# A planner's fetch rule and durations in a fused two-layer generator kernel

## The chip, the cores and the metric

The kernel runs on one core of a Trainium2 chip. The core has several engines that each work through a list of instructions of their own: TensorE (PE: matmuls, with PEld for the weight loads that overlap them), VectorE (DVE), ScalarE (ACT), GpSimd (POOL) and SyncE (SP, which here issues the DMA transfers). They wait for each other through semaphores. The metric is the time of one execution on the device in microseconds (us); lower is better.

## What is computed

Two layers over 1024 latent tokens and 256 context tokens, 1024 channels wide. Each layer normalises and modulates its input, projects it, runs three branches (a Fourier mix F, differential attention A, a bidirectional state-space scan S behind a short convolution), gates them, merges them and adds the result to the stream. The reference, cut to this:

```python
for l in range(DEPTH):
    h_l = rmsnorm(x, norm_w[l]) * (1.0 + sc_l) + sh_l          # and h_c from the context
    (fu, fg, q, k, v, ag, z, xbc, dt, gates) = split(h @ w_in[l])
    s = einsum('bqhmd,bkhmd->bhmqk', q, k) * ATT_QK ** -0.5    # two maps per head
    p = softmax(s); a = p[:, :, 0] - lam * p[:, :, 1]
    att = rmsnorm(einsum('bhqk,bkhe->bqhe', a, v), subln_w) * (1.0 - lam_init)
    xbc = silu(depthwise_conv(xbc, conv_w, conv_b))            # five taps, then two scans
    y_f = (fourier_mix(fu) * silu(fg)) @ w_of
    y_a = (att * silu(ag)) @ w_oa
    y_s = rmsnorm(ssd * silu(z), ssd_norm_w) @ w_os
    g = sigmoid(gates)
    x = x + g_l * ((g[0] * y_f + g[1] * y_a + g[2] * y_s) @ w_out[l])
return rmsnorm(x, norm_f)
```

## The kernel before

**Numbers.** Each fp32 operand of a large product is split into an fp16 part and an fp16 remainder, and three fp16 matmuls add up one product (`acc3`). Tiles of 128 tokens by 128 channels meet in matmuls of 128x512 or 128x256, in one of eight PSUM banks.

**Weights.** There are 40 weight tiles in a layer (`fu01`, `qk0`, `x0`, `of0`, `g10` and so on), 80 in all, each fetched by `fetch` (its calls, like every instruction, are recorded under line 397 of the profile, a helper). A fetch has two halves. For each half a 512-KB load brings fp32 values into one of two `raw` buffers, and ACT squares them; the square's output is only scratch and is written into the weight buffer itself, so it must wait until the buffer's last reader is done. What counts is the sum of squares by row (`s1p`, `s1f` or `s1e`). DVE adds the two halves' sums into `b16`, PE adds these over the 128 rows with a one-column matmul against `ones` (`colsum`), DVE makes a power of two of it (`pow2`), and with this scale ACT writes the fp16 part and DVE the remainder (`split_weights`). Letters p, f and e behind `s1` and `b16` tell the three lists that are fetched in their own order: projections (p), output and merge weights (f), and the gates of the scan branch, `g20` to `g23` (e).

**Space.** A fetched half lies in one of eight buffers `w0` to `w7` (`self.wfree`), or in one of 28 larger arena slots `ar0` to `ar27` (`self.free`), which otherwise hold the activations. `done` gives a half back and calls `prefetch`, which decides what to fetch next. Before the change a tile goes to arena slots only if it belongs to the next layer (`ahead`) or is one of `wo0` to `wo3`, the four tiles of the output weight.

**Order.** The kernel is written as six interleaved lists: m (the branches' own work), p (projections), f (merges and the output step), e (gates of the scan branch, behind all others in priority, so used as filler), g (modulation) and w (weight fetches). A planner in the kernel (`Scheduler`) runs through them once when the program is built. It keeps a clock for each engine, gives each instruction a duration (`cost`) and each pair of engines a lag, and each time issues the instruction that can start first, by priority where several can. What it issues is the order in which each engine then runs. DMA transfers have a model of their own: 475 ns of SP for the issue, at least 1100 ns plus bytes by a rate (360 per ns, 290 for a transpose) to the end, one after the other. `may_place` limits how many PSUM banks a list holds.

**The attention step.** For one tile of 128 queries and one head: scores matmuls into five banks, row maxima on DVE, exponentials on ACT, both maps combined on DVE and ACT to an fp16 pair, a transpose by DMA (`DMA_TRANSPOSE ar<-ar`, on SP's queue), and 30 values matmuls of 128x128 out of the transposed tiles.

**The convolution.** Its input comes from PSUM, ACT makes the first tap, DVE adds four more, ACT and DVE make the activation, and fp32 transposes on PE (`ps<-k,ar`, with the identity in `k`) turn the result for the scan.

Of the kernel before, what the change touches and what calls it, by code (L numbers as in the profile page):

```python
# [18 lines left out]
DRAM = bass.MemoryType.DRAM  # L19
# [47 lines left out]
ESIZE = {F32: 4, I32: 4, F16: 2, BF16: 2}  # L67
# [83 lines left out]
class Scheduler:  # L151
# [54 lines left out]
    def may_place(self, b):  # L206

        n, pend = self.count, self.pending
        keep = 0
        if b.th != 'w':  # L210
            if b.th != 'm' and pend['m']:
                keep += max(0, LEAST[self.barred != set()] - n['m'])
            if b.th != 'p' and pend['p'] + pend['w'] and not n['p'] + n['w']:
                keep += 1
        return self.order[b.th][0] is b and (n[b.th] < MAXB[b.th] or not any(pend[k] for k in 'mpf' if k != b.th)) and len(self.psum) > keep


    def cost(self, eng, name, outs, ins, kw, args):
        n = max(a.free_size() for a in outs + ins)
        if eng == 'PE':  # L220
            if name != 'matmul':
                return args[1].free_size() * NS_PE * 2 + 3.0
            n = args[2].free_size() * NS_PE
            return 3.0 + (n if ESIZE[ins[0].dtype] == 2 else max(4 * n, 213.0))
        if eng == 'ACT':
            aps = len(ins) - 1
            return (51 if ins[0].space == PSUM else 93) + n * NS_ACT + 93 * (aps + len(outs) - 1)
        if eng == 'DVE':
            fast = name == 'tensor_copy' or name == 'tensor_scalar'
            fast = fast and all(a.space != PSUM for a in outs + ins)  # L230
            scal = sum(a.free_size() == 1 for a in ins[1:]) if name in ('tensor_scalar', 'scalar_tensor_tensor') else 0
            return 68 + n * NS_DVE * (0.5 if fast else 1) + 61 * scal
        return 60.0 if name != 'tensor_copy' else 150.0 + 2 * n

    def add(self, eng, name, fn, args, kw):
# [19 lines left out]
        o.tail = 0.0  # L255
        if eng == 'SP':
            a = outs[0]
            o.tail = a.partition_size() * a.free_size() * ESIZE[a.dtype] / (720.0 if ins[0].space != DRAM and a.space != DRAM and name == 'dma_start' else 360.0 if name == 'dma_start' else 290.0)
        self.n += 1
        o.th, o.prio, o.n = self.cur, self.n - self.bias[self.cur], self.n  # L260
# [67 lines left out]
    def step(self):  # L328
# [52 lines left out]
        dur = o.dur  # L381
        self.now = s
        if e == 'SP':
            self.clock[e] = s + 475
            o.end = self.dma = max(self.dma, s + 1100) + o.tail
        else:
            if e == 'PE':
                w = int(s / GATE)
                if w != self.gate[0]:
                    self.gate = [w, 0.0, self.gate[1] if w == self.gate[0] + 1 else 0.0]  # L390
                if self.gate[2] < 0.5 * GATE:
                    dur *= 2
                self.gate[1] += dur
            o.end = self.clock[e] = s + dur
# [20 lines left out]
class Builder:  # L415
    def __init__(self, ctx, tc, A, out, dbg):
# [16 lines left out]
        self.wnext = {k: [(l, n) for l in range(2) for n in v] for k, v in (('p', W_PROJ), ('f', W_MERGE), ('e', W_GATE))}  # L433
        self.ev = set()
        self.block = {}
        self.cur, self.budget, self.held, self.cap = 'p', 0, 0, 99


# [118 lines left out]
    def fetch(self, k):  # L557

        nc = self.nc
        cur, ncur = self.cur, nc.cur  # L560
        self.cur, nc.cur = k, 'w'
        l, name = key = self.wnext[k].pop(0)
        self.whold[k] += 1
        halves, bufs = [], []
        sq = self.small(2)
        raws = []
        for j in range(2):
            if self.wfree:
                buf = self.wfree.pop(0)
                w = self.wbuf[buf]  # L570
            else:
                buf = self.alloc(keep=True)
                self.wborrow += 1
                w = buf.v16(2048).rearrange("p (a c) -> p a c", a=2)
            bufs.append(buf)
            halves.append((w[:, 0], w[:, 1]))
            raw = self.ring("raw", RAW, 1024)
            nc.sync.dma_start(raw, self.A['wt'][l, TILE_IDX[name]][:, j * 1024:j * 1024 + 1024])
            nc.scalar.activation(w[:, 1], raw, AF.Square, accum_out=sq[:, j:j + 1])
            raws.append(raw)  # L580
        inv = self.col("iw", 12)
        self.split_weights(halves, raws, sq, inv)
        self.wcache[key] = [halves, inv, bufs, k]
        nc.close('w')
        self.cur, nc.cur = cur, ncur

    def prefetch(self, want=None):

        idle = self.block.get('f') in {(l, 'z' + b) for l in range(2) for b in ORDER[1:]}
        for k in 'pef' if idle else 'pfe':  # L590
            while self.wnext[k] and self.wnext[k][0][0] < (self.layers if k == 'p' else min(self.layers, self.flayer + 1)):
# [1 line left out]
                ahead = k == 'p' and self.wnext['f'] and l > self.wnext['f'][0][0]  # L593
                left = k == 'f' and self.wnext['e'] and self.wnext['e'][0][0] == l
                lim = 1 if ahead else (0 if idle else 2) if left else WLIM[k] if (self.fetch_p if k == 'p' else self.fetch_f) else 0
                wo = name[:2] == 'wo'
                need = 2 + max(0, self.later) + (0 if (l, name) == want else BOR if wo and self.wborrow < BMAX else 99)
                borrow = (ahead or wo) and len(self.free) >= need
                if self.whold[k] >= lim or len(self.wfree) < 2 and not borrow:
                    break  # L600
                self.fetch(k)
# [4 lines left out]
    def done(self, L, name, half=None):  # L606

        e = self.wcache[L.l, name]
        for j in (0, 1) if half is None else (half,):
            if e[2][j] is not None:  # L610
                if isinstance(e[2][j], int):
                    self.wfree.append(e[2][j])
                else:
                    e[2][j].drop()
                    self.wborrow -= 1
                e[2][j] = None
        if e[2] == [None, None]:
            self.whold[e[3]] -= 1
# [1474 lines left out]
```

## Time and profile before

| | before |
|---|---|
| median of three runs | 2670.93 us |
| the three runs | 2670.9, 2670.93, 2677.07 us |
| the profiled execution's own time | 2677.08 us |
| its span, first to last instruction | 2675.3 us |
| mean granted PE clock | 0.979 |

The profile is of one execution, with times from the span's start. Each row of a timeline gives the start, the length, the engine, the operation, the tile written and the tiles read, and in brackets how long the engine had been idle before it and who ended that. Buffer numbers are left out: `ps<-ar,w` is any PSUM bank written from any arena slot and weight buffer. The waits of an engine are the same idle times, added up by who ended them. Consecutive rows of one kind are merged, with their count. The clock is a share of full speed; PE runs at either half or full speed, and the share of a stretch is the mean of the two.

### The profile page before, as it was taken

The numbers are of one execution on the slowest core, as the hardware profiler recorded it, in microseconds if no ns is written. First come the engines' busy times: TensorE is split into PE (matmuls) and PEld (weight loads), VectorE is DVE, ScalarE is ACT, GpSimd is POOL, SyncE is SP. The second block draws the span as 40 slices with busy tenths as digits, with TensorE's granted clock in tenths as the row PEclk, the third lists the DMA queues.
The fourth block names the chain that finished last, engine by engine and source line by source line (L and its number), as shares of the span: only waits on it lengthen the run. The fifth ranks groups of instructions, "written<-read, shape, count | busy, mean of one in ns | idle before, by whom it ended". The sixth has DMA issues, their size and how long they took to land. (4 is left out here: it accounts for less than half of the span.)

```text
span 2675.3 us, 42496 instructions
## 1 busy us (share of the span) xinstructions
PE 2516.4 (94%) x16962; PEld 1564.6 (58%) x16962; DVE 1829.7 (68%) x3783; ACT 1248.8 (47%) x2260; POOL 33.5 (1%) x78
## 2 busy tenths in 40 slices
PE   7999999999988998999999999999899899999998
PEld 3556655565564475476578546556545456566467
DVE  6785676666678487378566677766686649658476
ACT  4543535436355363363433464554554546345331
POOL 0000000000000000000000000000000000000000
PEclk8999999999999999999999999999999999999999
DMA  6311443324244222122542022433343322212451
GB/s 250 126 62 52 110 125 92 99 74 113 53 138 120 105 93 73 52 96 70 213 189 87 25 97 74 101 83 85 81 116 75 101 86 81 71 64 91 138 220 64
DMA packets 256978, 270.61 MB, mean 101 GB/s; under 512 B 181062, under 2 KB 191110, under 8 KB 256780
## 3 DMA queue, kind: packets, MB, share of 16 engines
q1 hardware_dynamic: 256780, 267.89, 33.2%
q8 instruction: 133, 2.18, 0.3%
q14 instruction: 65, 0.53, 0.1%
HBM read 178.02 MB, written 36.88 MB: 80 GB/s over the span
## 5 line engine op out<-in xcount | busy, mean ns | idle before, releaser
L397 PE MATMUL ps<-ar,w 128*128 128x512 f16 (+1 forms) x7968 | 1627.2, 357 | 13.9 <-ACT w L397 11.1
L397 PEld LDWEIGHTS <-w 128*128 128x128 f16 x7968 | 775.8, 99 | 740.9 <-issue 49.6
L397 PEld LDWEIGHTS <-ar 128*128 128x128 f16 x7376 | 592.2, 98 | 230.1 <-issue 54.9
L397 PE MATMUL ps<-ar,ar 128*128 128x128 f16 (+4 forms) x3652 | 404.2, 259 | 45.9 <-DMA ar<-ar 24.3
L397 PE MATMUL ps<-w,ar 128*128 128x256 f16 x3312 | 398.8, 273 | 0.0
L397 DVE TENSOR_REDUCE s1m<-ps 128x1 f32<-128x1280 f32 (+1 forms) x144 | 197.2, 1369 | 127.7 <-PE ps L397 127.0
L397 ACT ACTIVATE ar<-ps,s1m,qksc 128x1280 f32<-128x1280 f32 (+1 forms) x144 | 190.2, 1321 | 188.5 <-DVE s1m L397 144.0
L397 ACT ACTIVATE w<-raw 128x1024 f16<-128x1024 f32 x158 | 166.2, 1052 | 207.3 <-PE ps L397 117.6
L397 ACT ACTIVATE ar<-ar 128x1280 f16<-128x1280 f32 (+5 forms) x140 | 153.7, 1099 | 89.1 <-DVE ar L397 82.2
L397 DVE SCALAR_TENSOR_TENSOR ar<-ar,pv,ar 128x1284 f32<-128x1284 f32 x64 | 99.4, 1553 | 75.1 <-ACT ar L397 74.2
L397 DVE TENSOR_TENSOR ar<-ar,ar 128x1280 f16<-128x1280 f32 (+3 forms) x116 | 123.6, 1066 | 16.2 <-ACT ar L397 15.5
L397 PE MATMUL ps<-scrm,ar 128*128 128x64 f32 (+1 forms) x720 | 122.8, 307 | 9.9 <-DVE scrm L397 4.5
L397 ACT ACTIVATE ar<-ps 128x128 f32<-128x128 f32 (+6 forms) x196 | 70.1, 388 | 131.6 <-PE ps L397 129.3
L397 ACT ACTIVATE ar<-ps,ds 128x512 f32<-128x512 f32 (+1 forms) x88 | 54.8, 623 | 153.2 <-PE ps L397 153.2
L397 PEld LDWEIGHTS ps<-scrm,ar 128*128 128x128 f32 x720 | 99.5, 199 | 37.8 <-DVE scrm L397 19.6
L397 ACT ACTIVATE scrf<-ps,ds 128x512 f32<-128x512 f32 (+1 forms) x80 | 51.2, 639 | 120.7 <-PE ps L397 74.8
L397 DVE SCALAR_TENSOR_TENSOR ar<-ar,s1m,ar 128x1280 f32<-128x1280 f32 (+1 forms) x72 | 103.1, 1432 | 0.1
L397 PE MATMUL ps<-k,ar 128*128 128x128 f32 (+2 forms) x540 | 84.6, 282 | 18.9 <-DVE ar L397 17.9
L397 DVE SCALAR_TENSOR_TENSOR w<-raw,s1p,w 128x1024 f16<-128x1024 f32 x72 | 90.0, 1279 | 14.4 <-ACT w L397 14.3
L397 ACT ACTIVATE ar<-ar,ar 128x128 f32<-128x128 f32 x288 | 87.7, 387 | 15.7 <-DMA ar<-rows 15.7
L397 PEld LDWEIGHTS ps<-k,ar 128*128 128x128 f32 (+1 forms) x540 | 66.7, 156 | 47.2 <-DVE ar L397 29.5
L397 DVE SCALAR_TENSOR_TENSOR w<-raw,s1f,w 128x1024 f16<-128x1024 f32 x70 | 87.5, 1279 | 8.2 <-ACT w L397 8.2
(211 smaller groups left out, 2011.2 us busy)
## 6 DMA issues: line engine op xcount, KB each, us to landing
raw<-in_wt SPq DMA_DIRECT2D x160, 512.0 KB, 4.7
ar<-in_wm SPq DMA_DIRECT2D x48, 512.0 KB, 6.6
ar<-rows SPq DMA_DIRECT2D x36, 512.0 KB, 5.2
yp<-scrf SPq DMA_DIRECT2D x64, 256.0 KB, 2.0
ar<-in_x SPq DMA_DIRECT2D x20, 512.0 KB, 9.9
gs<-scre SPq DMA_DIRECT2D x32, 256.0 KB, 2.3
scrf<-yp SPq DMA_DIRECT2D x32, 256.0 KB, 2.7
ar<-ar SPq DMA_DIRECT2D x32, 160.0 KB, 2.8
```

The lines of the kernel that those rows point to most:

```text
L397: o.fn(*(place(a) for a in o.args), **{k: place(a) for k, a in o.kw.items()})
```

## The change

All four edits are in the planner and the fetch rule; both programs hold the same instructions.

1. `may_place`: a list that has its number of banks may take another one only if none of the lists m, p, f **and e** has work pending (before, e did not count).
2. `cost`: an fp16 matmul is planned with at least 25 ns, an fp32 one with 4n + 3, at least 223 ns (before 3 + max(4n, 213)).
3. DMA: loads of the kernel's inputs (`in_...`) and transposes end later for whoever waits for them, by 1000 and 900 ns (`late`); a transpose holds SP for 3040 ns (before 475).
4. `prefetch`: a tile of the running layer (no `wo`) may go to arena slots when at least six are free, nothing is held back (`self.later`) and fewer than four halves lie there for this reason (`self.spare`). Of the `wo` tiles only `wo0` and `wo1` may still borrow by the old rule.

```diff
-        return self.order[b.th][0] is b and (n[b.th] < MAXB[b.th] or not any(pend[k] for k in 'mpf' if k != b.th)) and len(self.psum) > keep
+        return self.order[b.th][0] is b and (n[b.th] < MAXB[b.th] or not any(pend[k] for k in 'mpfe' if k != b.th)) and len(self.psum) > keep
...
-            return 3.0 + (n if ESIZE[ins[0].dtype] == 2 else max(4 * n, 213.0))
+            return max(3.0 + n, 25.0) if ESIZE[ins[0].dtype] == 2 else max(4 * n + 3.0, 223.0)
...
             a = outs[0]
+            o.late = 1000.0 if ins[0].space == DRAM and ins[0].tensor.name[:3] == 'in_' else 900.0 if name != 'dma_start' else 0.0
+            o.issue = 475.0 if name == 'dma_start' else 3040.0
...
         if e == 'SP':
-            self.clock[e] = s + 475
-            o.end = self.dma = max(self.dma, s + 1100) + o.tail
+            self.clock[e] = s + o.issue
+            self.dma = max(self.dma, s + 1100) + o.tail
+            o.end = self.dma + o.late
...
+        self.spare = 0
...
             else:
                 buf = self.alloc(keep=True)
                 self.wborrow += 1
+                self.spare += 1
...
-                wo = name[:2] == 'wo'
+                wo = name in ('wo0', 'wo1')
                 need = 2 + max(0, self.later) + (0 if (l, name) == want else BOR if wo and self.wborrow < BMAX else 99)
                 borrow = (ahead or wo) and len(self.free) >= need
+                if not ahead and name[:2] != 'wo' and not self.later and (k != 'p' or l <= self.flayer) and self.spare < 4 and len(self.free) >= 6:
+                    borrow = True
                 if self.whold[k] >= lim or len(self.wfree) < 2 and not borrow:
                     break
...
                     e[2][j].drop()
                     self.wborrow -= 1
+                    self.spare -= 1
```

What this does to the order shows at three places. In the rows below a number behind an underscore tells one tile from another; `ps_63` is PSUM.

**The fetch of layer 0's gate tile `g11`**, behind layer 0's attention. In the order before, ACT's row with a `raw` source and an `s1f` output squares the tile's second half into `w2`; around it is the work of the scan and the convolution.

```order
L397 ACTIVATE ar9_73<-ps_63 128x128
L397 ACTIVATE ar11_75<-ps_63,ds_522 128x512 x2
L397 ACTIVATE w2_94,s1f_151<-raw_148 128x1024
L397 ACTIVATE ar11_75<-ps_63,ds_522 128x256
L397 ACTIVATE ar2_66<-ar11_75,pv0_142 128x1284
L397 ACTIVATE w2_94<-raw_148,s1f_151 128x1024
```

On PE, in the order before, the tile's one-column matmul (`b16f`, `ones16`) stands right behind the last matmul that reads the old contents of `w2`.

```order
L397 MATMUL ps_63<-ar25_89,w2_94 128x256
L397 LDWEIGHTS w2_94
L397 MATMUL ps_63<-ar25_89,w2_94 128x256
L397 LDWEIGHTS ones16_141
L397 MATMUL ps_63<-b16f_152,ones16_141 128x1
L397 LDWEIGHTS w2_94
L397 MATMUL ps_63<-ar16_80,w2_94 128x512
```

In the order after, ACT squares the tile's halves into `w6` and into the arena slot `ar6`, one behind the other.

```order
L400 ACTIVATE ar12_76<-ps_63 128x128
L400 ACTIVATE ar27_91<-ps_63 128x128
L400 ACTIVATE w6_98,s1f_151<-raw_148 128x1024
L400 ACTIVATE ar6_70,s1f_151<-raw_148 128x1024
L400 ACTIVATE ar11_75<-ps_63,ds_475 128x512
L400 ACTIVATE w6_98<-raw_148,s1f_151 128x1024
```

On PE, in the order after, the one-column matmul stands 916 operations earlier than before, amid matmuls on another tile, `w1`.

```order
L400 MATMUL ps_63<-ar17_81,w1_93 128x512
L400 LDWEIGHTS w1_93
L400 MATMUL ps_63<-ar17_81,w1_93 128x512
L400 LDWEIGHTS ones16_141
L400 MATMUL ps_63<-b16f_152,ones16_141 128x1
L400 LDWEIGHTS w1_93
L400 MATMUL ps_63<-ar18_82,w1_93 128x512
```

So the fetch has left the place where its own buffer comes free.

**The values matmuls of an attention tile** (layer 0, first head, third tile). In the order before, PE has between the last scores matmul (`ar3`, `ar15`) and the first values matmul (`ar12`, `ar10`) seven merge matmuls on the weight buffer `w7`, of which the first and the last are shown.

```order
L397 MATMUL ps_63<-ar3_67,ar15_79 128x256
L397 LDWEIGHTS w7_99
L397 MATMUL ps_63<-ar21_85,w7_99 128x512
...
L397 MATMUL ps_63<-ar25_89,w7_99 128x512
L397 LDWEIGHTS ar10_74
L397 MATMUL ps_63<-ar12_76,ar10_74 128x128
```

In the order after there are eleven, five on `w7` and six on `w4`, from `ar10`, `ar15` (scores) to `ar24`, `ar6` (values).

```order
L400 MATMUL ps_63<-ar10_74,ar15_79 128x256
L400 LDWEIGHTS w7_99
L400 MATMUL ps_63<-ar23_87,w7_99 128x512
...
L400 MATMUL ps_63<-ar22_86,w7_99 128x512
L400 LDWEIGHTS w4_96
L400 MATMUL ps_63<-ar9_73,w4_96 128x512
...
L400 MATMUL ps_63<-ar7_71,w4_96 128x512
L400 LDWEIGHTS ar6_70
L400 MATMUL ps_63<-ar24_88,ar6_70 128x128
```

The values matmuls have moved back by four matmuls.

**The output step of layer 1.** In the order before, PE passes from the first output block (`ar9` the merged stream, `w3` half of the output weight) over the one-column matmul of the next output tile to the second block (`ar15`, `w1`).

```order
L397 MATMUL ps_63<-w3_95,ar9_73 128x256
L397 LDWEIGHTS ones16_141
L397 MATMUL ps_63<-b16f_152,ones16_141 128x1
L397 LDWEIGHTS ar9_73
L397 MATMUL ps_63<-w3_95,ar9_73 128x256
L397 LDWEIGHTS ar15_79
L397 MATMUL ps_63<-w1_93,ar15_79 128x256
```

In the order after, PE goes from the first block (`ar18`, `w5`) to 33 matmuls of the last gate tile (`ar17` half of `g23`, `ar26` the layer's input), and then to the second block (`ar4`, `w6`). The last row of each piece is followed by more of its kind.

```order
L400 MATMUL ps_63<-w5_97,ar18_82 128x256
L400 LDWEIGHTS ar18_82
L400 MATMUL ps_63<-w5_97,ar18_82 128x256
L400 LDWEIGHTS ar17_81
L400 MATMUL ps_63<-ar26_90,ar17_81 128x512
...
L400 MATMUL ps_63<-ar13_77,ar17_81 128x512
L400 LDWEIGHTS ar4_68
L400 MATMUL ps_63<-w6_98,ar4_68 128x256
```

Half of the gate tile has moved into the output step. The first five output blocks there stop after 21 of their 24 matmuls and finish later, after the eighth channel piece of the merged stream, which needs these gates.

## Rows read from the trace of the kernel before

**Rows 1.** The page's busy us of each engine, its share of the span, instructions:

```profile
PE 2516.4 (94%) x16962; PEld 1564.6 (58%) x16962; DVE 1829.7 (68%) x3783; ACT 1248.8 (47%) x2260; POOL 33.5 (1%) x78
```

**Rows 2.** Granted clock of the core:

```profile
core 0: 2675.3 us, clock 0.979
```

**Rows 3.** Three stretches: length, PE, PEld, DVE, ACT, POOL busy, clock, DMA:

```profile
0.00:50.00 50.00, 32.46 (x121) 14.09 (x122) 30.23 (x76) 19.95 (x33) 0.55 (x5) 0.83 0.85 334
1050.00:1100.00 50.00, 36.37 (x183) 18.96 (x182) 24.53 (x27) 17.52 (x38) 0.00 (x0) 0.86 0.13 44
2550.00:2600.00 50.00, 49.90 (x322) 31.01 (x320) 41.03 (x77) 20.77 (x29) 0.00 (x0) 1.00 0.62 244
```

**Rows 4.** What PE waited for: us in total, times, longest us:

```profile
PE ps L397 <- DMA ar<-ar: 24.3, 34, 2.8
PE ps L397 <- DVE ar L397: 21.4, 14, 9.1
PE ps L397 <- DVE b16p L397: 19.9, 14, 2.9
PE ps L397 <- DVE b16f L397: 16.2, 14, 2.8
PE ps L397 <- DMA ar<-in_wm: 15.2, 4, 7.4
PE ps L397 <- ACT ar L397: 11.6, 11, 2.2
PE ps L397 <- ACT w L397: 11.1, 6, 4.2
PE ps L397 <- DVE b16e L397: 7.3, 3, 4.4
PE ps L397 <- DVE s1m L397: 5.9, 11, 0.7
```

**Rows 5.** PE's groups by shape: busy us, mean ns, idle before by releaser:

```profile
L397 PE MATMUL ps<-ar,w 128*128 128x512 f16 x6144 | 1432.7, 382 | 13.7 <-ACT w L397 11.1 <-DVE ar L397 1.8 <-DVE w L397 0.8
L397 PE MATMUL ps<-w,ar 128*128 128x256 f16 x3312 | 398.8, 273 | 0.0
...
L397 PE MATMUL ps<-k,ar 128*128 128x128 f32 x426 | 71.9, 294 | 18.9 <-DVE ar L397 17.9 <-DVE scrp L397 0.2
```

**Rows 6.** Timeline, reused buffer: start us, us, instruction, [idle before]:

```profile
1775.82 1.03 PE L397 MATMUL ps<-ar,w 128*128 128x512 f16 x4
...
1776.89 1.06 ACT L397 ACTIVATE w<-raw 128x1024 f16<-128x1024 f32 x1 [2.21 <-PE ps L397]
...
1778.28 0.16 PE L397 MATMUL ps<-b16p,ones 128*128 128x1 bf16 x1 [1.43 <-DVE b16p L397]
```

**Rows 7.** Timeline of a fetch whose load came late:

```profile
801.08 1.06 ACT L397 ACTIVATE w<-raw 128x1024 f16<-128x1024 f32 x1 [1.97 <-DMA raw<-in_wt]
...
802.48 0.16 PE L397 MATMUL ps<-b16p,ones 128*128 128x1 bf16 x1 [2.88 <-DVE b16p L397]
```

**Rows 8.** Timeline of the last such fetch:

```profile
2496.89 0.16 PE L397 MATMUL ps<-b16f,ones 128*128 128x1 bf16 x1 [1.32 <-DVE b16f L397]
```

**Rows 9.** Timeline around the largest gap, at a convolution of layer 0:

```profile
1052.97 6.32 DVE L397 SCALAR_TENSOR_TENSOR ar<-ar,pv,ar 128x1284 f32<-128x1284 f32 x4
...
1062.24 2.38 PE L397 MATMUL ps<-k,ar 128*128 128x128 f32 x8 [9.11 <-DVE ar L397]
```

**Rows 10.** Timeline at the end of layer 1's attention:

```profile
2087.82 1.42 ACT L397 ACTIVATE ar<-ps,s1m,qksc 128x1280 f32<-128x1280 f32 x1 [2.69 <-PE ps L397]
...
2100.18 1.85 PE L397 MATMUL ps<-ar,ar 128*128 128x128 f16 x30 [0.68 <-DMA ar<-ar]
```

**Rows 11.** DMA issues: count, KB each, median us from issue to landing:

```profile
raw<-in_wt SPq DMA_DIRECT2D x160, 512.0 KB, 4.7
...
ar<-gs SPq DMA_DIRECT2D x8, 512.0 KB, 8.3
...
ar<-ar SPq DMA_TRANSPOSE x72, 4.9
```

## The prediction

> **What bounds the kernel now.** I read the engines' busy shares first, then the clock by stretches, then what TensorE (PE) waits for, and last the stretches around its larger gaps. PE is busy 2516.4 of 2675.3 us, 94% [rows 1], while DVE has 68% and ACT 47%. The change keeps every instruction and its shape (15,976 matmuls and 444 transposes in either order), so PE's work stays. What a new order can move is the 158.9 us in which PE idles, and the clock. The mean granted clock of 0.979 [rows 2] means that about 56 us are lost to the lower of its two levels (2675.3 x 0.021). Of these, 8.5 lie in the first 50 us, where it is 0.83 [rows 3], and some 4 in the tail. That leaves about 44 us in the middle, in stretches after gaps, such as 1050 to 1100 us with 0.86 [rows 3]. The last stage before the tail isn't waiting at all: PE 49.90 of 50 us there [rows 3].
>
> Of the idle time 134 us lie between start and tail. PE's waits sort them by releaser [rows 4]: 24.3 us for the transposing DMA ahead of the values matmuls of attention, 19.9 + 16.2 + 7.3 = 43.4 us for the three `b16` tiles (the sums of squares of a weight tile, which a one-column matmul must add up before the tile can be scaled), 11.1 us for weight tiles that ACT had not scaled yet, and 21.4 for `ar` tiles from DVE, of which 17.9 precede the `ps<-k,ar` transposes behind the SSD convolution [rows 5]. 15.2 us belong to `in_wm` at the start.
>
> **The change part by part.** Durations come from the profiled execution: span 2675.3, time 2677.08, so 1.8 us lie outside. It is the longest of the three runs; their median is 6.2 us less. The sum is made against 2677.1.
>
> *Transposes, 24.3 us in 34 waits, mean 0.71.* The cost model's SP entry for a transpose rises from 475 to 3040 ns and its end by 900 ns. The trace's landing is 4.9 us [rows 11]. In the order before, the commonest number of matmuls between the last scores matmul and the first values matmul is 7 (the mean is 2.63 us of work); now it is 11 (mean 3.26). A 128x512 matmul takes 1432.7 / 6144 = 0.233 us [rows 5] (busy time by count, since matmuls overlap), so four more are 0.93 us for the commonest case, 0.63 us in the mean. That is about the mean wait, but the longest wait was 2.8 [rows 4]. Bounds: 0 (the wait came from a late DVE result, not from the DMA) and -24.3. I take **-16**, near the full end because 0.63 to 0.93 stands against 0.71.
>
> *Reused buffers, 14.1 us in eight of the 31 `b16` gaps.* Six of them are 1.43 us each. [rows 6] shows one: PE's last matmul on a weight buffer ends at 1776.85, the ACT square of the next tile, which writes into that buffer, starts at 1776.89, takes 1.06, and after DVE's addition PE goes on at 1778.28. PE has nothing in between because its next instruction is that very one-column matmul. Arena slots (and the earlier fetch) break this loop when a free one is there. Counting the PE work between a buffer's last reader and the next tile's one-column matmul, eight tiles had under 0.5 us before; now three (layer 1's `z0`, `z1`, `g23`). At one step of 1.43 to 1.8 us each, and with `z0`, `z1`, `g23` staying, I take **-9**; bounds -14.1 and 0.
>
> *Late weight loads, 15.2 us in eleven of the 31 `b16` gaps.* Here the square itself waited for `raw<-in_wt`; the largest is 2.88 us and the last 1.32 [rows 7, 8]; four of the eleven are under 0.7. The model ended such a load 3.5 us after its issue, now 4.5; the trace has 4.7 [rows 11]. One microsecond covers the four small ones (2.4 in all) and shortens the other seven by 1.0 each: **-9**, bounds -15.2 and 0. [...]
>
> *The scaling behind a late sum.* PE waits 11.1 us for tiles that ACT has not scaled [rows 4], all behind the gaps above. Where the tile comes earlier this goes too; three stay: **-7** (bounds -11.1, 0).
>
> *The convolution, 17.9 us.* From the last convolution matmul to the first transpose ACT and DVE need a copy, an ACT step, four DVE steps of together 6.32 us [rows 9], and another step of ACT and of DVE of 1.3 to 1.5 each, about 12.5 us with the hops. Whatever PE work stands between covers it. Summing the work between in the twelve places: six fall short of 12.5, by 7.7, 4.2, 2.6, 1.2, 3.2 and 0.3, 19.2 in all, near the 17.9 of [rows 5]. In the new order the same count gives 11.6 (4.0, 2.9, 2.1 and five smaller). The 9.11-us gap [rows 9], where the weight splits of `g10` stood in DVE's way too, had 8.3 us of cover and gets 16.8. So **-7**; bounds -17.9 and +8, since covers of 8.5 to 10.4 now stand in places that had 15 to 21.
>
> *The clock.* The terms so far take 48 of the 134 us of middle gaps; the same share of 44 us is 16. Short gaps such as the 1.43 ones may have cost none. I take **-13** (bounds 0 and -25).
>
> *What gets worse.* (a) At the end of layer 1's attention the merge matmuls that fill have been used earlier (the merge of branch 0 ends 619 PE operations sooner). Between the last scores and the last values matmuls stand 8.1 us of work, 16.6 before. From the last exponentials to the values matmuls 12.4 us pass [rows 10], with 1.6 of a weight's work in them; with the reduction ahead the chain is some 13.5. A stall of **+5**, and **+2** of clock. (b) The last gate tile of layer 1 is now used inside the output step: 33 gate matmuls stand between the first output block and the next, and the blocks behind wait for gates that go out to `gs` and return, 8.3 us for the load [rows 11]. 91 matmuls of 0.120 us (398.8 / 3312, [rows 5]) cover 10.9 us of 11 to 17: **+3**, bounds 0 and +6; the cover that is gone was a stage with no idle time [rows 3]. (c) At the start one more tile is fetched and all of group 2's transposes come ahead of the first projection: **+2** (bounds 0, +4). (d) Everything else is reordered too, and PE's smaller waits (11.6 for ACT's `ar`, 5.9 for `s1m` [rows 4]) can grow as well as shrink: **+8**, nearly half of what these two hold now, bounds -5 and +20.
>
> What costs nothing: the borrowing's counter and the gate's PSUM rule add no instruction; the wider fp16 cost (25 ns at least) acts on one-column matmuls alone.
>
> Sum: -16 -9 -9 -7 -7 -13 = -61; +5 +2 +3 +2 +8 = +20; together **-41**. 2677.1 - 41 = 2636 for the profiled execution, and 2670.9 - 41 = **2630** on the median, which is the figure given.
>
> **The rivals.**
> 1. *The gaps only move.* The filler matmuls are the same in number; to give a transposing DMA four more, another place must go without. For it: covers at the convolution and the attention's end do fall. Against it: each half-layer still has a hundred or more merge matmuls left at its end, and the fetches at last readers are gone, not displaced. If two thirds of the -61 return elsewhere: -20 + 20 = 0, **2671**, with 10 to either side.
> 2. *Slower: layer 1 runs out of filler.* One mechanism, from the end of layer 1's attention through its six convolution blocks: merge matmuls spent earlier leave bare covers. Were each of the six to stall like the 9.11 us of [rows 9], it is 55 us against 4.7 counted before, +50; the clock in such a stretch is 0.86, 7 us of 50 [rows 3], some +15 more. With the attention's end: -41 + 65 = +24, **2695**. It decides from a cover of 5 us or less per block; my count has 8.5 at the least, which speaks against it.
> 3. *Full gain.* The bounds of the first four terms reached, with the clock's 25: -24 -14 -15 -11 -7 -25 + 12 = -84, **2587**.
> 4. *Landing grows.* More fetches lie earlier, among other loads: 512-KB loads of `gs` land after 8.3 us where the queue is full [rows 11]. If weight loads went from 4.7 to that, the eleven late ones would be 3.6 longer, +40 in place of -9: 2630 + 49 = **2679**. [...] Against it: only two raw buffers exist, so no more than one tile's loads are under way at any time, as before.
> 5. *The borrowing does nothing*, because six free slots are never there. The new order has borrowed tiles (both halves of `oa1`, halves of `g11`, `g10`, `g20`), so this one has next to no chance.
>
> **How the numbers follow.** 0.3% is about what a measurement of this kernel tells from no change; faster means below 2663, slower above 2679. Forecast (2600 to 2655) 0.58; gaps only move 0.17, of which a third lies under 2663, most of the rest is the same; slower by lost filler 0.09; full gain 0.12; landing 0.04, half of it the same. Faster: 0.58 + 0.12 + 0.07 = 0.77; same 0.12; slower 0.11. The range 2590 to 2673 leaves out about 6 in 100 below and 14 above.
>
> **What would show it.** PE's waits for `DMA ar<-ar` at 8 us or less; the `b16` waits at 20 to 25; no gap near 9 us at the transposes of the convolution; the clock at 0.984 or more. (a) shows as a wait of about 5 us for the last values matmuls, at 2090 or so; (b) as PE idle behind the first output block near 2540. The forecast is wrong if the waits for DVE's `ar` grow past 30, or if the `b16` waits stay at 40 while buffers are free: then the sums were late for ACT's order, not for buffers or loads.

## The result, and the profile after

| | before | after |
|---|---|---|
| median of the runs | 2673.10 us (2670.9 to 2677.07) | 2615.05 us (2614.21 to 2615.48) |
| profiled execution, own time | 2677.08 us | 2615.48 us |
| its span | 2675.3 us | 2613.7 us |
| PE busy | 2516.4 us | 2501.8 us |
| PE idle (span less busy) | 158.9 us | 111.9 us |
| mean granted PE clock | 0.979 | 0.980 |

The changed kernel is faster: ratio 0.9781, 95% interval 0.9764 to 0.9798. It gained 58 us of median, 61.6 between the two profiled executions; the forecast was 41, its range held the time. The median before is of four executions (the three of the section above and one of 2675.26 us); the profiled one is the slowest of them.

The page's line of engines, which answers to [rows 1]:

```profile
PE 2501.8 (96%) x16962; PEld 1565.2 (60%) x16962; DVE 1828.2 (70%) x3783; ACT 1252.1 (48%) x2260; POOL 33.7 (1%) x78
```

PE's waits (us in total, times, longest), which answer to [rows 4]:

```profile
PE ps L400 <- DVE ar L400: 26.2, 12, 10.4
PE ps L400 <- DMA ar<-in_wm: 15.3, 5, 7.6
PE ps L400 <- ACT ar L400: 14.5, 15, 3.8
PE ps L400 <- DVE b16p L400: 9.7, 10, 1.6
PE ps L400 <- DMA ar<-ar: 9.4, 9, 1.9
PE ps L400 <- ACT w L400: 6.1, 4, 4.2
PE ps L400 <- DVE b16e L400: 5.0, 4, 2.0
...
PE ps L400 <- DVE scrm L400: 3.2, 9, 0.9
...
PE ps L400 <- DVE b16f L400: 1.6, 3, 0.7
```

The wait for the transposing DMA fell from 24.3 to 9.4 us. The three `b16` rows together fell from 43.4 to 16.3. The wait for weight tiles fell from 11.1 to 6.1, and the one for `s1m`, 5.9 before, is gone. The row of DVE's `ar` grew from 21.4 to 26.2, and its longest wait is 10.4 us. Most of it stands in one form, the fp32 transposes on PE, which answers to the last of [rows 5] (busy us, mean ns, idle before):

```profile
L400 PE MATMUL ps<-k,ar 128*128 128x128 f32 x426 | 74.2, 303 | 27.6 <-DVE ar L400 25.9 <-DVE scrp L400 0.9 <-DVE s1g L400 0.2
```

25.9 us of waits for DVE, 17.9 before. The longest stand in three places. The first is the start; here PE's timeline (start, length, instruction, idle before):

```profile
67.42 3.64 PE L400 MATMUL ps<-k,ar 128*128 128x128 f32 x16 [10.40 <-DVE ar L400]
70.85 9.81 PE L400 MATMUL ps<-ar,w 128*128 128x512 f16 x44
```

The kernel before had 35 projection matmuls ahead of these transposes and waited for 1.82 us:

```profile
59.26 7.86 PE L397 MATMUL ps<-ar,w 128*128 128x512 f16 x35 [1.82 <-DVE ar L397]
```

The second is a convolution of layer 0:

```profile
880.07 0.47 PE L400 MATMUL ps<-k,ar 128*128 128x128 f32 x1 [5.67 <-DVE ar L400]
```

The third is the end of layer 1's attention, which answers to [rows 10]:

```profile
2064.09 1.88 PE L400 MATMUL ps<-ar,ar 128*128 128x512 f16 x6 [3.84 <-ACT ar L400]
2067.87 3.36 PE L400 MATMUL ps<-ar,ar 128*128 128x128 f16 x30 [1.90 <-DMA ar<-ar]
2073.27 0.16 PE L400 MATMUL ps<-b16e,ones 128*128 128x1 bf16 x1 [2.04 <-DVE b16e L400]
2076.46 0.90 PE L400 MATMUL ps<-k,ar 128*128 128x128 f32 x3 [3.03 <-DVE ar L400]
```

Three stretches (length, busy us of PE, PEld, DVE, ACT, POOL, then clock, DMA share, GB/s) show the clock at these places:

```profile
50.00:100.00 50.00, 38.31 (x247) 23.83 (x245) 39.58 (x97) 31.39 (x51) 0.00 (x0) 0.86 0.16 49
850.00:900.00 50.00, 43.77 (x229) 23.10 (x228) 19.63 (x29) 23.93 (x47) 0.00 (x0) 0.90 0.23 74
2050.00:2100.00 50.00, 39.06 (x262) 24.15 (x261) 35.42 (x62) 33.32 (x58) 0.30 (x5) 0.86 0.39 101
```

The kernel before had 1.00 in all three, here the first and the last of them:

```profile
50.00:100.00 50.00, 47.19 (x323) 29.24 (x323) 43.24 (x111) 33.34 (x56) 0.00 (x0) 1.00 0.13 42
2050.00:2100.00 50.00, 44.95 (x307) 24.38 (x305) 31.77 (x51) 28.66 (x45) 0.24 (x3) 1.00 0.42 98
```

Its last values matmuls stand 16 us later there (2100.18, 2084.51), but from 2100 to 2150 us both kernels have 0.93. Elsewhere the clock rose: 1050 to 1100 us went from 0.86 to 1.00, and 800 to 850 from 0.90 to 1.00. Read in pieces of half a microsecond, the traces show two levels: of the 5350 pieces of the kernel before 5105 have 1.00, 206 have 0.50 and 39 lie between; of the changed kernel's 5226 it is 5013, 187 and 26. In the output step PE's timeline goes from the 33 gate matmuls over 91 output matmuls to a wait of 0.41 us:

```profile
2514.10 7.29 PE L400 MATMUL ps<-ar,ar 128*128 128x512 f16 x33
2521.23 10.10 PE L400 MATMUL ps<-w,ar 128*128 128x256 f16 x91
2531.74 30.52 PE L400 MATMUL ps<-w,ar 128*128 128x256 f16 x278 [0.41 <-ACT ar L400]
```

### The profile page after: what moved, and what is told of

It reads as the page before. It is cut to its first block, busy times and chain, and to the rows that moved or that the text cites. A ratio compares the mean times of both kernels' runs of the same rounds, so it can differ in the third digit from the quotient of the medians.

```text
span 2613.7 us, 42499 instructions
## 1 busy us (share of the span) xinstructions
PE 2501.8 (96%) x16962; PEld 1565.2 (60%) x16962; DVE 1828.2 (70%) x3783; ACT 1252.1 (48%) x2260; POOL 33.7 (1%) x78
## 5 line engine op out<-in xcount | busy, mean ns | idle before, releaser
L400 PE MATMUL ps<-ar,w 128*128 128x512 f16 (+1 forms) x7200 | 1463.1, 356 | 9.4 <-ACT w L400 6.1
L400 PEld LDWEIGHTS <-w 128*128 128x128 f16 x7200 | 699.5, 98 | 643.0 <-issue 20.3
L400 PEld LDWEIGHTS <-ar 128*128 128x128 f16 x8144 | 668.1, 98 | 256.7 <-issue 36.7
L400 PE MATMUL ps<-ar,ar 128*128 128x128 f16 (+4 forms) x4420 | 555.9, 277 | 24.7 <-ACT ar L400 14.1
L400 ACT ACTIVATE w<-raw 128x1024 f16<-128x1024 f32 x145 | 152.4, 1051 | 128.1 <-PE ps L400 75.3
L400 ACT ACTIVATE ar<-ar 128x1280 f16<-128x1280 f32 (+4 forms) x140 | 153.8, 1100 | 102.0 <-DVE ar L400 91.8
L400 PE MATMUL ps<-k,ar 128*128 128x128 f32 (+2 forms) x540 | 88.6, 292 | 27.6 <-DVE ar L400 25.9
L400 DVE SCALAR_TENSOR_TENSOR ar<-ar,ps 128x512 f32<-128x512 f32 (+1 forms) x116 | 64.3, 562 | 65.1 <-ACT ar L400 47.8
L400 PEld LDWEIGHTS ps<-k,ar 128*128 128x128 f32 (+1 forms) x540 | 68.8, 163 | 61.6 <-DVE ar L400 31.0
L400 ACT ACTIVATE ar<-ar,ar 128x128 f32<-128x128 f32 x288 | 88.1, 388 | 24.3 <-DMA ar<-rows 21.0
L400 DVE SCALAR_TENSOR_TENSOR w<-raw,s1p,w 128x1024 f16<-128x1024 f32 x71 | 89.1, 1279 | 11.3 <-ACT w L400 11.2
```

The costliest lines, as they stand in the source:

```text
L400: o.fn(*(place(a) for a in o.args), **{k: place(a) for k, a in o.kw.items()})
```

## The experiments

Twelve kernels were run. "Idle" is span less PE's busy time, "clock" is the span times the missing share of the granted clock, both of the profiled execution; the next columns are PE's waits for the transposing DMA, for the three `b16` tiles and for ACT's `ar`. Ratios are to executions of the kernel before from the same round (medians 2673.3 to 2676.4 us; for the changed kernel 2673.1), with the 95% interval. A profile is of one execution: e9's ran 6.5 us below its kernel's median, e5's 5.4 above, so a few us of idle time or clock between two rows tell nothing.

| kernel | edits in it | median us | ratio | idle | clock | DMA `ar` | `b16` | ACT `ar` |
|---|---|---|---|---|---|---|---|---|
| before | none | 2673.1 | | 158.9 | 56 | 24.3 | 43.4 | 11.6 |
| after | all | 2615.1 | 0.9781 (0.9764, 0.9798) | 111.9 | 52 | 9.4 | 16.3 | 14.5 |
| e1_trans | transpose: SP 3040, late 900 | 2653.4 | 0.9918 (0.9900, 0.9935) | 140.1 | 61 | 4.4 | 43.1 | 17.0 |
| e2_late_in | inputs late 1000 | 2659.6 | 0.9940 (0.9924, 0.9956) | 146.0 | 53 | 31.9 | 23.5 | 11.5 |
| e3_borrow | borrowing, PSUM rule | 2688.5 | 1.0052 (1.0036, 1.0067) | 164.4 | 67 | 27.5 | 34.8 | 38.9 |
| e4_mp | PSUM rule | 2671.1 | 0.9986 (0.9973, 0.9998) | 157.1 | 48 | 23.7 | 44.0 | 9.0 |
| e5_no_borrow | all but borrowing | 2628.4 | 0.9837 (0.9819, 0.9855) | 125.3 | 58 | 6.6 | 27.4 | 9.9 |
| e6_no_trans | all but transpose | 2693.2 | 1.0073 (1.0055, 1.0091) | 169.7 | 81 | 22.3 | 14.3 | 54.4 |
| e7_no_in | all but inputs | 2599.4 | 0.9727 (0.9706, 0.9747) | 108.9 | 34 | 8.9 | 30.4 | 4.1 |
| e8_pe16 | all, old fp32 cost | 2589.1 | 0.9688 (0.9672, 0.9705) | 95.7 | 36 | 3.0 | 13.2 | 13.4 |
| e9_trans_late | transpose: late 900 only | 2646.1 | 0.9896 (0.9880, 0.9911) | 134.7 | 47 | 6.4 | 40.1 | 14.8 |
| e10_borrow_no_e | as e3, not for list e | 2646.1 | 0.9896 (0.9878, 0.9914) | 145.7 | 29 | 24.5 | 46.6 | 17.7 |
| e11_issue2600 | as e8, SP 2600, `wo` by the old rule | 2614.4 | 0.9780 (0.9760, 0.9799) | 109.5 | 44 | 6.4 | 19.0 | 15.2 |
| e12_issue2800 | as e8, SP 2800, `wo` by the old rule | 2588.7 | 0.9683 (0.9668, 0.9697) | 95.9 | 34 | 3.8 | 14.2 | 12.0 |

### One edit at a time

**Transposes.** The edit on the kernel before, without the lines that use the two numbers, which are those of the change. e1 has both numbers; e9 has the lateness alone (SP's entry stays 475):

```diff
+            o.late = 0.0 if ins[0].space == DRAM and ins[0].tensor.name[:3] == 'in_' else 900.0 if name != 'dma_start' else 0.0
+            o.issue = 475.0 if name == 'dma_start' else 3040.0
...
```

> The kernel before with one edit: a transpose is planned with 3040 ns of SP and an end 900 ns later; no other duration, no borrowing. Theory (each edit takes away the wait it aims at, and the gains add up): in the order, the work between last scores and first values matmul is under 1.9 us in 12 of 72 places instead of 50, so the wait for DMA ar<-ar falls from 24 us to 8 or less, the late weight loads stay, and the time falls by 15 to 25 us, to about 2652. Rival 1 (any new order is as good as another; the targeted wait is only moved): the wait for DMA ar<-ar falls, others rise by as much, 2665 to 2680. Rival 2 (the edits pay only together): under 8 us of gain.

> The kernel before with only the 900 ns of lateness of a transpose; SP's 475 ns stay. The order has 17 of 72 values steps under 1.9 us (50 before), and everything else that I count is as before: eight reused buffers, 19.5 us of shortfall at the convolution. Theory (the matmuls ahead of the values matmuls are what the transposes' edit is worth): DMA ar<-ar falls from 24 to 8 us, the other waits stay, 2650 to 2662. Rival (what the first experiment gained came from its other changes, 3040 ns of SP): 2665 to 2680.

Measured: e1 2653.4, e9 2646.1, 4 us under its range. PE's waits of e9:

```profile
PE ps L400 <- DVE b16f L400: 17.9, 17, 2.1
...
PE ps L400 <- DVE b16p L400: 15.7, 13, 1.9
...
PE ps L400 <- DVE b16e L400: 6.5, 3, 2.7
PE ps L400 <- DMA ar<-ar: 6.4, 7, 1.7
```

The wait for the DMA is 6.4 us, and the `b16` rows (with `b16e`'s 6.5, 40.1) stayed. That is the aimed-at wait taken away, 18 us of it, with its neighbours nearly left alone; idle time as a whole fell by 24 us and the clock's loss by 9. The 3040 ns of SP add nothing that can be seen without the other edits: e1, which has them, isn't faster than e9.

**Inputs.** `o.late = 1000.0` for tensors `in_...`, nothing else.

> The kernel before with one edit: loads of the kernel's inputs are planned to end 1000 ns later. Theory: the b16 waits (43 us) lose the late loads, 9 us or more, and here also half of the reused buffers (4 tiles instead of 8 have under 0.5 us between last reader and one-column matmul), while the wait for DMA ar<-ar stays at 24: 2650 to 2662. Rival 1: the b16 waits fall but come back elsewhere, 2665 to 2680. Rival 2: under 8 us of gain.

```profile
PE ps L400 <- DMA ar<-ar: 31.9, 34, 6.0
...
PE ps L400 <- DVE b16p L400: 10.3, 9, 2.4
PE ps L400 <- DVE b16f L400: 7.5, 8, 2.0
...
PE ps L400 <- DVE b16e L400: 5.7, 2, 4.2
```

PE's waits, again: the `b16` rows add up to 23.5 us, 20 less than before, somewhat more than was expected (9 for the late loads and half of the 14 for reused buffers); the DMA row, expected to stay, rose to 31.9. The time is 14 us down, as expected.

**Borrowing.** Edit 4 with edit 1, all durations as before; and edit 1 alone.

> The kernel before with the borrowing rule and the PSUM rule in may_place, without any change of durations. Theory: the reused-buffer loops go (3 tiles instead of 8), b16 waits fall by some 15 to 43 - 15 = 28 us, late loads stay, DMA ar<-ar falls little (42 of 72 places stay under 1.9 us), the convolution's shortfall goes from 19 to 5 us: 2640 to 2655. If the long stall near 67 us of the changed kernel comes from the early borrowed fetch, it is here too. Rival 1: 2665 to 2680, waits moved. Rival 2: under 8 us of gain.

> The kernel before with the PSUM rule in may_place alone. Theory: it frees no buffer and knows no duration, so nothing that counts changes: the same within 8 us of the kernel before. Rival 1 (the order itself is what scatters): it moves by more than 8 us, either way, with waits of all kinds.

e4 is within 0.3% of before. e3 is some 14 us slower by its ratio, against the theory and past rival 1's bound. (Without edit 1 the planner comes to a point with borrowed tiles where it may issue nothing, so the borrowing is run with it throughout.) Its wait for ACT's `ar`, and the stretch near the end of layer 0's attention:

```profile
PE ps L397 <- ACT ar L397: 38.9, 20, 6.1
```

```profile
800.00:850.00 50.00, 26.11 (x136) 13.91 (x135) 43.49 (x54) 17.35 (x29) 0.88 (x4) 0.64 0.46 135
```

PE is busy for 26.11 of 50 us there, at a clock of 0.64; before it was 35.52 at 0.90:

```profile
800.00:850.00 50.00, 35.52 (x217) 19.23 (x216) 41.77 (x83) 29.14 (x55) 0.54 (x8) 0.90 0.54 150
```

From 775 to 850 us PE has in e3 not one matmul on a weight buffer: the attention's scores and values stand there without filler. In e3's order all four gate tiles of list e (`g20` to `g23`) lie at least by half in arena slots in layer 0; over both layers ACT squares 17 halves into arena slots (2 before), 10 of them list e's. The first of the four comes earlier than before, the others later. PE's one-column matmuls on `b16e` stand at 115, 584, 923 and 1132 us in layer 0, at 341, 533, 773 and 835 before. The third, in e3 and before:

```profile
923.13 0.16 PE L397 MATMUL ps<-b16e,ones 128*128 128x1 bf16 x1 [0.38 <-DVE b16e L397]
```

```profile
773.28 0.16 PE L397 MATMUL ps<-b16e,ones 128*128 128x1 bf16 x1 [1.43 <-DVE b16e L397]
```

The filler's second tile is used up by 775 us, just ahead of the starved stretch, and the third comes when layer 0's attention is over; the kernel before has it at 773 us, with tiles of the attention still to come. So the filler is spent early, and what should follow it is late; which of the two weighs more, no run here tells apart. e10 forbids list e to borrow:

```diff
-                if not ahead and name[:2] != 'wo' and not self.later and (k != 'p' or l <= self.flayer) and self.spare < 4 and len(self.free) >= 6:
+                if not ahead and name[:2] != 'wo' and not self.later and k != 'e' and (k != 'p' or l <= self.flayer) and self.spare < 4 and len(self.free) >= 6:
```

> The borrowing and the PSUM rule without any durations, as in the third experiment, but the gate tiles g20 to g23 (list e) may not borrow. Theory (the borrowing alone was slower because these tiles came early and their matmuls, the filler, were spent before the end of layer 0's attention; ACT's ar took 39 us of waits there): that wait falls back to about 12 us, and the time to 2650 to 2668, under the kernel before. Rival (borrowing without right durations is worth nothing, whatever the tiles): 2672 to 2690.

```profile
PE ps L397 <- ACT ar L397: 17.7, 16, 2.2
...
PE ps L397 <- DVE ar L397: 11.3, 11, 2.3
```

```profile
800.00:850.00 50.00, 38.08 (x225) 20.54 (x225) 41.57 (x82) 29.77 (x56) 0.50 (x7) 0.83 0.53 143
```

The wait for ACT's `ar` is 17.7 us, not 38.9, the stretch has 38.08 us at 0.83, and the time is 2646.1: 42 us better than e3 and 4 under the expected range. So what made the borrowing slow was list e's part in it. e10 says less about the rest of the borrowing: it squares only 6 halves into arena slots, the first at 894 us, so the stretch above has nearly the order of the kernel before. That may be why the `b16` rows, 46.6 us, did not fall; e10's gain lies in the waits for DVE's `ar` (11.3, 21.4 before) and in the clock (29 us lost, not 56), and which of its changed places made it was not tried.

### One edit left out

> The changed kernel without the borrowing (edits 1 to 3 alone). Theory A (the borrowing, 14 us slower when alone, is worth something once the durations are right, because the reused-buffer loops stay without it: 6 tiles under 0.5 us against 4 in the changed kernel, and one of them then stands behind each bad cover): 2632 to 2648. Theory B (all of the gain is the durations', the borrowing is worth nothing): within 8 us of the changed kernel, 2607 to 2623. In both the stall of some 10 us near 67 us stays, since the order of the start is the same.

> The changed kernel with the old durations of a transpose (475 ns of SP, no lateness). Theory A (the edits need each other: with the old durations the filler is spent too early in the attention, as in the borrowing alone; the covers of the last six tiles of layer 0's attention are 0 for four of them): the gain shrinks by far more than the 22 us of the transposes alone, 2650 to 2685, with ACT's ar as a large wait near 800 us. Theory B (gains add up): 2632 to 2642.

> The changed kernel with the old durations of input loads (no lateness of 1000 ns). If gains add up: the 16 us of that edit alone are lost, 2626 to 2636, and the b16 waits rise from 16 to 27 us or more with ACT waiting for raw. If the borrowing already covers late loads: within 8 us, 2607 to 2623.

e5, without the borrowing, is 13 us slower than the changed kernel: between the two theories' ranges, and nearer A's. Its `b16` waits are 27.4 us against 16.3, so the borrowing takes waits away as A says; the waits for weight tiles that ACT had not scaled (15.4 against 6.1) do as much. Its stall at the start is as long as the changed kernel's, with no borrowed tile:

```profile
66.64 3.65 PE L400 MATMUL ps<-k,ar 128*128 128x128 f32 x16 [10.40 <-DVE ar L400]
```

e6, without the transposes' durations, is 78 us slower than the changed kernel and 20 slower than before, which is theory A and more. PE's waits and the stretch from 750 us:

```profile
PE ps L400 <- ACT ar L400: 54.4, 19, 6.3
...
PE ps L400 <- DMA ar<-ar: 22.3, 32, 2.1
```

```profile
750.00:800.00 50.00, 22.98 (x131) 14.29 (x130) 42.27 (x50) 17.31 (x27) 0.00 (x0) 0.60 0.46 126
```

22.98 us busy of 50, clock 0.60. The borrowing without the transposes' durations starves the attention again, with the sign that e3 has: 12 of the 13 halves in arena slots are list e's, and the `b16e` matmuls of layer 0 stand at 120, 903, 1117 and 1342 us. In the changed kernel they stand at 122, 544, 771 and 817, the first as early, the others where before had them, and the attention isn't starved. The edits do not add up.

e7, without the inputs' lateness, misses both figures: it is 16 us *faster* than the changed kernel, although the aimed-at waits, the `b16` rows, did rise as expected, to 30.4 us. Its idle time is nearly the changed kernel's (108.9 and 111.9). The difference is the clock, 34 us lost against 52. From 2050 to 2250 us, e7 first, then the changed kernel:

```profile
2050.00:2250.00 200.00, 186.76 (x1120) 115.04 (x1118) 143.00 (x284) 113.08 (x219) 1.05 (x17) 0.98 0.31 94
```

```profile
2050.00:2250.00 200.00, 181.29 (x1072) 114.18 (x1071) 136.51 (x271) 102.55 (x206) 1.02 (x17) 0.92 0.26 78
```

0.98 against 0.92 is 12 us in these 200. e7 has ten waits there, 12.8 us with the longest 4.7, and the changed kernel eleven, 18.3 us, where four of 1.9 to 3.8 us follow each other within 17 us. Why an edit that is worth 14 us alone costs 16 here is not settled beyond this; the kernel e8 without it was not tried.

### The start, and the end of layer 1's attention

The order of the changed kernel's start comes from 7 ns: an fp32 matmul of 128 columns is planned with 223 ns, not 216. e8 takes that back and keeps all else.

```diff
-            return max(3.0 + n, 25.0) if ESIZE[ins[0].dtype] == 2 else max(4 * n + 3.0, 223.0)
+            return max(3.0 + n, 25.0) if ESIZE[ins[0].dtype] == 2 else 3.0 + max(4 * n, 213.0)
```

> The changed kernel with the old cost of fp32 matmuls (7 ns less for a 128-column one); the fp16 floor and all else stay. The order at the start then has 48 projection matmuls ahead of the last group's transposes again, as before the change. Theory (the 10.4-us stall near 67 us and its low clock of 0.86 come from that order, not from the early extra fetch, which stays in place): the wait there falls to 2 us, the clock in 50 to 100 us is 1.00, some 15 us; the cover at the end of layer 1's attention is 17 us again, not 8, and the convolution's shortfall 3 us, not 12: another 10 us. 2588 to 2602. Rival (the stall is the DVE's load with the extra fetch, and stays): 2607 to 2623.

```profile
59.68 7.86 PE L400 MATMUL ps<-ar,w 128*128 128x512 f16 x35 [1.81 <-DVE ar L400]
```

```profile
50.00:100.00 50.00, 47.74 (x330) 29.59 (x329) 44.86 (x115) 33.94 (x58) 0.00 (x0) 1.00 0.15 53
2050.00:2100.00 50.00, 46.68 (x287) 25.29 (x286) 37.13 (x63) 34.61 (x64) 0.00 (x0) 1.00 0.44 128
```

The wait is 1.81 us again, with 35 projection matmuls behind it, and the stretch has 47.74 us busy at 1.00, where the changed kernel has 38.31 at 0.86. All fourteen profiles agree: the four kernels with the new fp32 duration (the changed one, e5, e6, e7) wait 10.1 to 10.4 us there and have 0.86 from 50 to 100 us, the ten others wait 1.8 and have 1.00. The end of layer 1's attention is at 1.00 as well. The time is 2589.1 us, 26 less than the changed kernel, at the faster end of what was expected: the best with e12. The extra fetch stays in e8, so it wasn't the cause.

To price the end of layer 1's attention apart from the start, e11 and e12 change SP's 3040 ns in e8 to 2600 and 2800. Both also give the `wo` tiles their old rule back, which their expectations leave out; at 3040 ns this alone leaves the planner's order of e8 as it is, and e11 and e12 share it. The first gives a layer 1 much like the changed kernel's behind e8's start.

> The 2589-us kernel (all edits, old fp32 cost) with 2600 ns of SP for a transpose instead of 3040. Its start is that kernel's, its layer 1 is nearly the changed kernel's: 8.0 us of work ahead of the last values matmuls of layer 1's attention instead of 17.2, the convolution blocks there with 8.5 to 12.4. Theory (that place costs what the changed kernel's trace shows, some 10 us of waits at 2064 to 2111 and 10 us of clock): 2600 to 2612, with those waits and a clock of 0.86 to 0.93 there. Rival (the stall in the changed kernel followed from its start or layer 0): 2585 to 2595.

> The same with 2800 ns. The count gives 14.7 us ahead of the last values matmuls of layer 1, 2.0 us of shortfall at the convolution (3.4 in the 2589-us kernel), four reused buffers as there. If these counts carry the time: 2582 to 2592, the fastest. If what they leave out matters as much: 2592 to 2605.

```profile
2062.83 2.04 PE L400 MATMUL ps<-ar,ar 128*128 128x512 f16 x6 [3.63 <-ACT ar L400]
...
2075.13 0.90 PE L400 MATMUL ps<-k,ar 128*128 128x128 f32 x3 [3.03 <-DVE ar L400]
```

```profile
2050.00:2100.00 50.00, 38.88 (x260) 23.93 (x259) 35.65 (x61) 32.32 (x57) 0.31 (x5) 0.86 0.39 94
```

e11 has the changed kernel's gaps at this place (3.63 and 3.03 of five), its clock of 0.86, and 2614.4 us: 25 more than e8, somewhat over what was expected. The two orders differ in other places too (e11 waits 12 us longer for DVE's `ar`, of which about 5 lie here), so 25 is the price of the whole order and not of this place. Between e11 and e12 only the number differs: 200 ns of it are worth 26 us. e12 is level with e8, as its counts said.

## Why the prediction was right, and where it was off

Its sign and range held, and the waits that it aimed at are those that fell. The terms were off by more than the total shows, by up to 14 us each and both ways, so that the total came so near is in part luck. It is more so as small changes of one duration move the order, and the time with it, by as much: 26 us for 7 ns (e8), 16 for e7, 26 between e11 and e12. In its order:

- **Transposes**, forecast -16: from 24.3 to 9.4, -14.9. The step holds. e9 and e6 show the same wait going and coming with the transposes' durations (6.4 with the 900 ns alone, 22.3 with all edits but the transposes').
- **Reused buffers and late loads**, forecast -9 and -9: the `b16` rows fell by 27.1. The loads' term was too small. I took one microsecond off each late load; e2, the lateness alone, took 20 us off, and with the other edits it takes 14 (e7 to after). That fetches planned later also come away from their buffers' last readers fits the count in e2's expectation (4 such tiles, not 8). The buffers' term is of the right size with the other durations (e5 to after, 27.4 to 16.3) and by itself (e3, 43.4 to 34.8, though its time rose); e10, which borrows little, has 46.6.
- **Scaled tiles**, forecast -7: 11.1 to 6.1, -5.0.
- **The convolution**, forecast -7: without the 10.40 us at the start, 25.9 is 15.5, so -2.4. The count named the places but not the lengths: the gap of 9.11 us is gone, one of 5.67 us has come at 880 us.
- **The clock**, forecast -13, and +2 with (a): the loss went from 56 to 52 in the two profiles, and by all executions it did not move: 27 later ones of the kernel before have 0.977 to 0.984, median 0.981, the changed kernel's four 0.980 to 0.982. The step that failed is taking a share by idle time: e7 loses 34 us with the changed kernel's idle time, e10 29 with 146 us idle, e1 61 with 140. The change made new waits that cost clock, 7 us at the start, 5 at 880 us and 7 around 2064 to 2076. Long waits aren't the only ones that do: in e1, behind waits of 2.1, 3.1 and 1.6 us in the scan of layer 1, 25 us have 0.59, which is 10 us lost (shown behind this list). That short gaps such as the 1.43 ones cost none doesn't hold either for the one of [rows 6]: 1775 to 1785 us of the kernel before have 0.83.
- **(a) The end of layer 1's attention**, forecast +5 and +2: the waits from 2079 to 2108 us were 9.3 before, those from 2060 to 2111 are 14.6 after, +5.3; the clock's part was +7, not +2. The size is right, the place is not: the last values matmuls (2084.51) don't wait at all. PE waits before them: for ACT ahead of the last scores, for the transposing DMA of the tile before, for a weight's sum and at a convolution.
- **(b) The output step**, forecast +3: PE waits 0.41 us there. The 91 matmuls take 10.10 us, so the chain took some 10.5, an estimate from these two rows, just under the 11 to 17 of the prediction's.
- **(c) The start**, forecast +2 with +4 as the bound: 10.40 against 1.82 us, and 7 us of clock (0.14 of 50). This term was priced without the cover that it moved: 44 projection matmuls of 0.233 us are 10.3 us, and they were put behind the transposes that wait for DVE. e8 gives it back. What put them there, the 7 ns of edit 2, has no term in the prediction; its list of what costs nothing names only the fp16 half of that edit.
- **(d) Everything else**, forecast +8: ACT's `ar` +2.9, `s1m` -5.9, `scrm` -2.3, together -5.3. The sign was wrong.

The stretch of e1:

```profile
2200.00:2225.00 25.00, 18.17 (x67) 12.84 (x67) 17.10 (x43) 11.19 (x25) 0.34 (x6) 0.59 0.19 64
```

The parts of the list overlap, since the waits of (a) stand in the rows of ACT's `ar`, the DMA, `b16` and DVE's `ar` too; they don't add up to the idle time.

Idle (-47.0) and clock (-4) make 51 of the 61.6 us; the other 11 are busy time that this clock figure doesn't account for. Busy time less the clock's loss lies between 2443 and 2470 us over the fourteen profiles; it is lowest where the loss is largest (e6, 81 us) and highest where it is smallest (e10, 29). That fits a figure that counts idle time at the lower level as lost too (in the changed kernel PE is busy for 0.00 us from 60 to 67 us, and the clock is 0.50); what is left of the 11 beyond that stays open.

Of the prediction's signs, the waits for `DMA ar<-ar` (9.4, not 8 or less) and the clock (0.980, not 0.984) missed, the `b16` waits fell further than said (16.3, not 20 to 25), and no gap near 9 us is left at a convolution. Neither sign of being wrong came: DVE's `ar` stayed under 30 (26.2), the `b16` waits didn't stay at 40.

Of the rivals, "the gaps only move" is refuted by the `b16` and DMA rows. The filler's rival was right as a mechanism but not as the likeliest place: it is what made e3 and e6 slower than before, at the end of layer 0's attention, where list e borrows and transposes are planned short. The full gain's 2587 is near the 2589 of e8 and e12, whose start no longer stalls and whose end of layer 1's attention waits less (the longest there 2.2 us in e8, 2.9 in e12); their terms aren't that rival's, though (e12's `b16` waits are 14.2 us and its clock's loss 34). "Landing grows" fell, by the median in the DMA issues of the changed kernel:

```profile
raw<-in_wt SPq DMA_DIRECT2D x160, 512.0 KB, 4.6
```

4.6 us after, 4.7 before [rows 11].

## What to carry to other kernels

A planner's wrong duration can show in the profile as many short waits behind one kind of operation; here setting that number nearer to the trace's removed most of that kind of wait (24.3 us to 6.4 in e9), and it could be tested alone. What it did to the time came out differently in each company (the loads' lateness: 14 us gained alone, 16 lost with the other edits), so test it with the others too. Space for early weights is not a gain by itself: when list e took most of it and transposes were planned short, the filler was missing at the end of the attention, and the place to look is the end of the stage. When a step moves work, price the cover that it takes from the place it leaves (count its matmuls), and look up the clock of that stretch: the 10-us wait at the start took 7 us of clock besides.

## What was not expected of the hardware

Nothing of the kind was new but the size of the clock's part: among the runs with 96 to 147 us of idle time, the loss to the lower level goes from 29 to 61 us, and e10 has the least clock loss (29) with 146 us of idle time, e1 the most of these (61) with 140. All four executions of each agree (0.988 to 0.990 for e10, 0.977 and 0.978 for e1).
